# A decoder layer on one core: two small PSUM tiles drawn from another pool

## Chip, cores and metric

One core of a Trainium2 chip runs the whole kernel as one launch. The metric is the device time of that core in microseconds (us), the median of several executions. Beside it one execution was recorded by the hardware profiler; all rows below are from that one.

## What is computed

One inference step of one decoder layer, for a prompt of 1024 tokens of width 1024 and for 8 sample tokens. The layer has two mixers side by side, then cross-attention and a feed-forward part:

```python
def layer(l, x, mem_k, mem_v, shift0, wkv0):
    y_mix, chunk_v, shift_new, wkv_new = parallel_mixer(rmsnorm(x, ...), shift0, wkv0, ...)
    x = x + y_mix
    x = x + cross_attn(rmsnorm(x, norm_x_g[l]), mem_k, mem_v, w_xq[l], w_xo[l])
    x = x + sq_relu_ffn(rmsnorm(x, norm_ffn_g[l]), w_up[l], w_down[l])
```

The change touches mixer B, a recurrence with a 64 by 64 state for each of 8 heads, whose outputs are normalised per head, given a bonus term and gated:

```python
def step(S, inp):
    r_t, d_t, k_t, v_t, kk_t, a_t = inp
    sa = jnp.einsum('bhvk,bhk->bhv', S, -kk_t)
    S = S * d_t[:, :, None, :] + sa[..., None] * (kk_t * a_t)[:, :, None, :] + v_t[..., None] * k_t[:, :, None, :]
    return S, jnp.einsum('bhvk,bhk->bhv', S, r_t)
yb = headnorm(yb, ln_g, ln_b, GN_EPS)
out_b = ((yb + bonus).reshape(bsz, L, D_B) * g)
```

## The kernel before

Phase 1 is both mixers, phase 2 the output projection, the attention and the feed-forward part. In phase 1 the prompt is taken in two halves of 512 tokens, and the 8 heads of mixer B in four pairs (`pr`), two pairs at a time (`q`). A half has 8 chunks of 64 tokens (`NCH`, `C`), and the recurrence is solved chunk by chunk with small products.

For each half and pair the stages are, by name:

- `rkv`, `kknorm` (tile `pss`), `decay` (tiles `psw`, `psa`) and `factors` make the scaled operands `st` and `bk`. The ScalarE step at L446 reads `psa` into `ta`, which has one buffer; the VectorE step at L472 in `factors` is the last reader of the previous `ta`.
- `gram` (L478) multiplies `bk` with `st` in two groups of four chunks. Each group needs two tiles `psgram` at once; VectorE reads one at L499 and the other at L502. A gram cannot start before `bk` is written (L473 on VectorE, L474 on GpSimd).
- `inverse`, `join` (tiles `ps_j`), `ends` (`pse`) and `values` (`psv`) follow; `join` gives `tt`.
- `fold` (L615) runs twice for each pair: 32 TensorE products of 64 by 64 into one tile `psf`, then two copies out of it. The first fold (`i` = 0) rewrites the chunk ends, the second (`i` = 1) rewrites half of `ab`, copied by ScalarE twice (L626).
- `chain` walks the state through the chunks (`psx`, `psz`).
- `outs` (L651) sums the outputs in two tiles `psy`, which are open from the first chunk of the chain to the last, and which VectorE then reads (L669, L671).
- `gn` (L686) is the output norm: after a ScalarE square (L693) and a reciprocal root (L155 to L158), GpSimd scales `y` (L697), TensorE transposes it into the tile `psgn` (L700), ScalarE reads that (L702), GpSimd adds the bonus (L703), TensorE makes the gate in the tile `psgate` (L705), and VectorE multiplies (L706).

PSUM has eight banks, and a tile here takes one. In phase 1 they are shared out as pools: `pg` (two, tag g: the large projections and some transposes), `pm` (two, tag m), `pc` (two, the chain) and `py` (two, tag y). `pm` serves `pss`, `psw`, `psa`, `psgram`, `ps_j1` and `ps_j2`. `py` serves `psb`, `psv`, `pse`, `ps_j3`, `psf`, `psy`, `psgn`, `psgate` and a few sample tiles. A tile whose pool has no free slot waits until the last reader of an older one is done.

The stages are written in the list `ORDER` (L39), which gives their priority. The context is opened with `schedule_with_timeline_sim=True` (L1659): a planner takes the priorities and a simulated timeline, lets work whose data and slot are there go ahead, and fixes one order of instructions for each engine. Each engine then works in that order. The part of `ORDER` around the first of the places discussed reads:

```python
chain 0 0 6 8, outs 0 0, proj_a 0 1 1, fold 0 1 1, factors 0 2, mix_a 0 0,
x_store 1 0, decay 0 3, norm_a 0 1, gram 0 2, outs 0 1, factors 0 3, gram 0 3, x_store 1 1, gn 0 0
```

The arguments are half, pair (or `q`), and a part: `fold 0 1 1` is the second fold of pair 1 in half 0.

Of the kernel before, what the change touches and what calls it, by code (L numbers as in the profile page):

```python
# [9 lines left out]
F32 = mybir.dt.float32  # L10
# [9 lines left out]
P = 128  # L20
# [8 lines left out]
C = 64  # L29
NCH = HALF // C  # L30
# [40 lines left out]
class K:  # L71
# [543 lines left out]
    def fold(self, hf, pr, i):  # L615

        nc, t = self.nc, self.s[pr]
        tt = t["tt"]
        ps = self.py.tile([P, NCH, C], F32, tag="y", name="psf")
        hrs = (slice(0, 64), slice(64, 128))  # L620
        dsts = [t["e"][hr, 0:NCH, h, :] if i == 0 else t["ab"][hr, :, C:] for h, hr in enumerate(hrs)]
        for c in range(NCH):
            for hr, dst in zip(hrs, dsts):
                nc.tensor.matmul(ps[hr, c, :], tt[hr, c, :], dst[:, c, :], start=True, stop=True)
        for h, (hr, dst) in enumerate(zip(hrs, dsts)):
            self.copy((("vector", "scalar"), ("scalar", "scalar"))[i][h])(dst, ps[hr])  # L626
# [59 lines left out]
    def gn(self, hf, pr):  # L686
        nc, s1, s2 = self.nc, self.s1, self.s2
        t = self.s[pr]
        y = t["y"]
        y3 = y.rearrange("p (g v) -> p g v", v=64)  # L690
        sq = self.sl.tile([P, HALF], F32, tag="gs", name="gs")
        v, rs, tmp = (s1.tile([P, 8], F32, tag=f"gn{n}", name=f"gn{n}") for n in ("v", "r", "t"))
        nc.scalar.activation(sq, y, AF.Square)  # L693
        nc.vector.tensor_reduce(v, sq.rearrange("p (g v) -> p g v", v=64), axis=AX.X, op=ALU.add)
        nc.vector.tensor_scalar(v, v, 1.0 / 64, GN_EPS, op0=ALU.mult, op1=ALU.add)
        self.rsqrt(v, rs, tmp)
        nc.gpsimd.tensor_tensor(y3, y3, rs.unsqueeze(2).broadcast_to([P, 8, 64]), op=ALU.mult)  # L697
        ps = self.py.tile([P, 4, P], F32, tag="y", name="psgn")
        for c in range(4):
            nc.tensor.transpose(ps[:, c, :], y[:, c * P:(c + 1) * P], self.ident)  # L700
        psf = ps.rearrange("p c t -> p (c t)")
        nc.scalar.activation(y, psf, AF.Identity, scale=self.g["rw_ln_g"][:, pr:pr + 1], bias=self.g["rw_ln_b"][:, pr:pr + 1])  # L702
        nc.gpsimd.tensor_tensor(y, y, t["bv"], op=ALU.add)  # L703
        psg = self.py.tile([P, 512], F32, tag="y", name="psgate")
        nc.tensor.matmul(psg, self.g2[:, pr * P:(pr + 1) * P], self.s["G0"], start=True, stop=True)  # L705
        nc.vector.tensor_tensor(y, y, psg, op=ALU.mult)  # L706
        nc.sync.dma_start(self.d_o[hf][4 + pr], y)
# [955 lines left out]
```

## Time and profile before

| | |
|---|---|
| median of 3 executions | 1791.45 us (1782.59 to 1793.16) |
| the profiled execution, its own time | 1794.84 us |
| its span, first to last instruction | 1793.1 us |
| mean granted TensorE clock | 0.949 of full speed |
| TensorE busy | 1634.6 us, 91% of the span |
| VectorE busy | 1221.3 us, 68% |
| GpSimd busy | 837.1 us, 47% |
| ScalarE busy | 781.1 us, 44% |

The profile writes PE for TensorE, PEld for its weight loads, DVE for VectorE, ACT for ScalarE, POOL for GpSimd and SP for SyncE; L624 is line 624 of the kernel. An arrow out<-in names the tile written and those read. A row of the timeline may merge several like instructions (x30). Behind a group or a row in square brackets stands the idle time of the engine ahead of it and what ended it.

### The profile page before, as it was taken

Reading aid. Unit: us, or ns where it says so; the run is one execution under the profiler, and the core shown is the slowest. Engines: PE = TensorE matmul, PEld = TensorE weight load, DVE = VectorE, ACT = ScalarE, POOL = GpSimd, SP = SyncE. Lnnn points to the kernel's source line nnn. Section 1 sums busy time; section 2 is a strip of 40 time slices with the busy share of each in tenths; the row PEclk is TensorE's granted clock in tenths of the full one; section 3 lists DMA queues with packets and bytes.
Section 4 is the critical chain, followed back from the end, with each engine's and each line's share of the span. In section 5 each row is a group of like instructions: output and inputs, shape, how many; then the busy total and the mean of one; then the engine's idle time right before and its main releaser. Section 6 shows DMA issues by size and latency. Waiting matters only on the chain. (4 is left out here: it accounts for less than half of the span.)

```text
span 1793.1 us, 38347 instructions
## 1 busy us (share of the span) xinstructions
PE 1634.6 (91%) x15379; PEld 1521.9 (85%) x15379; DVE 1221.3 (68%) x2300; ACT 781.1 (44%) x1467; POOL 837.1 (47%) x643
## 2 busy tenths in 40 slices
PE   6989868998897689998999889999999999999997
PEld 6878757886786578887988789999999989999997
DVE  5586687768757965656667365655655697877796
ACT  4535543455443234433344233444544564444442
POOL 5450152323146864466343178687754533222343
PEclk8999978999898889999999999999999999999998
DMA  4411423221122456555455342567644585555442
GB/s 139 118 37 58 124 69 93 83 57 52 53 76 73 131 172 196 174 169 175 144 184 165 139 130 82 167 201 225 195 155 142 186 281 184 156 142 153 137 125 107
DMA packets 248547, 244.28 MB, mean 136 GB/s; under 512 B 24937, under 2 KB 191233, under 8 KB 248369
## 3 DMA queue, kind: packets, MB, share of 16 engines
q1 hardware_dynamic: 248324, 241.82, 44.1%
q8 instruction: 121, 1.98, 0.5%
q14 instruction: 58, 0.47, 0.1%
q10 hardware_dynamic: 44, 0.01, 0.0%
HBM read 179.95 MB, written 61.83 MB: 135 GB/s over the span
## 5 line engine op out<-in xcount | busy, mean ns | idle before, releaser
L104 POOL TENSOR_TENSOR wl<-wst,wh 128x1024 fp32r<-128x1024 f32 x70 | 170.3, 2433 | 125.6 <-ACT wh L103 112.1
L1215 PE MATMUL ps_S<-c_o,wS 128*128 128x258 f32 x1536 | 226.4, 282 | 0.0
L1215 PE MATMUL ps_S<-c_cb,wS 128*128 128x258 f32 x1536 | 226.0, 282 | 0.0
L136 PE MATMUL ps_g<-xh,wh 128*128 128x256 f32 (+1 forms) x704 | 214.6, 305 | 5.4 <-ACT xr L288 1.8
L136 PE MATMUL ps_g<-xl,wh 128*128 128x256 f32 (+1 forms) x704 | 209.6, 298 | 0.5 <-DVE xl L104 0.5
L136 PE MATMUL ps_g<-xh,wl 128*128 128x256 f32 (+1 forms) x704 | 207.7, 296 | 0.0
L1215 PEld LDWEIGHTS ps_S<-c_cb,wS 128*128 128x128 f32 x1536 | 201.8, 189 | 0.0
L1215 PEld LDWEIGHTS ps_S<-c_o,wS 128*128 128x128 f32 x1536 | 201.8, 189 | 0.0
L136 PE MATMUL ps_g<-o,wh 128*128 128x260 f32 (+1 forms) x768 | 178.0, 325 | 14.5 <-DVE yq L1240 8.9
L1215 PE MATMUL ps_A<-c_cb,wA 128*128 128x258 f32 x1152 | 173.0, 284 | 7.6 <-ACT c_cb L103 3.9
L1215 PE MATMUL ps_A<-c_o,wA 128*128 128x258 f32 x1152 | 172.7, 284 | 0.0
L1215 PEld LDWEIGHTS ps_A<-c_cb,wA 128*128 128x128 f32 x1152 | 153.4, 190 | 8.8 <-ACT c_cb L103 4.3
L1215 PEld LDWEIGHTS ps_A<-c_o,wA 128*128 128x128 f32 x1152 | 153.2, 190 | 0.4 <-DVE c_o L104 0.4
L103 ACT CAST wh<-wst 128x1024 fp32r<-128x1024 f32 x92 | 96.1, 1046 | 130.5 <-PE ps_g L136 63.9
L136 PEld LDWEIGHTS ps_g<-o,wh 128*128 128x128 f32 x768 | 129.2, 191 | 27.6 <-issue 9.2
L136 PEld LDWEIGHTS ps_g<-xh,wh 128*128 128x128 f32 x704 | 140.3, 199 | 12.9 <-issue 5.0
L136 PEld LDWEIGHTS ps_g<-xl,wh 128*128 128x128 f32 x704 | 139.9, 199 | 5.6 <-issue 2.2
L136 PEld LDWEIGHTS ps_g<-xh,wl 128*128 128x128 f32 x704 | 139.2, 198 | 3.0 <-issue 1.4
L1171 POOL TENSOR_TENSOR rS<-wr,rS 128x512 f32<-128x512 f32 x48 | 70.4, 1467 | 121.9 <-DMA wr<-in_w_down_dram 61.7
L136 PE MATMUL ps_g<-o,wl 128*128 128x260 f32 (+1 forms) x384 | 123.5, 322 | 1.4 <-POOL wl L104 1.4
L103 ACT CAST wS<-rS 128x512 fp32r<-128x512 f32 x96 | 59.3, 620 | 144.1 <-POOL rS L1171 84.1
L104 DVE TENSOR_TENSOR wS<-rS,wS 128x512 fp32r<-128x512 f32 x96 | 81.9, 853 | 46.6 <-ACT wS L103 46.3
(493 smaller groups left out, 3877.2 us busy)
## 6 DMA issues: line engine op xcount, KB each, us to landing
hb<-d_h SPq DMA_DIRECT2D x105, 258.0 KB
wst<-in_w_in_dram SPq DMA_DIRECT2D x44, 512.0 KB
d_h<-ht SPq DMA_DIRECT2D x64, 258.0 KB
wr<-in_w_down_dram SPq DMA_DIRECT2D x26, 512.0 KB
d_h<-yq SPq DMA_DIRECT2D x48, 258.0 KB
wst<-in_w_out_dram SPq DMA_DIRECT2D x16, 512.0 KB
ck<-in_cache_mem_k_dram SPq DMA_DIRECT2D x32, 256.0 KB
ck<-in_cache_mem_v_dram SPq DMA_DIRECT2D x32, 256.0 KB
```

The lines of the kernel that those rows point to most:

```text
L103: (heng or nc.scalar.copy)(hi, src)
L104: (eng or nc.vector).tensor_tensor(lo, src, hi.bitcast(F32), op=ALU.subtract)
L136: nc.tensor.matmul(ps, l[:, k, :], r[:, cols], start=(k == 0 and i == 0), stop=(k == kt - 1 and i == 2))
L1171: nc.gpsimd.tensor_tensor(R[n], R[x], R[y], op=op)
L1215: nc.tensor.matmul(ps[:, s], l[:, i, :], r[:, c, cols], start=k == 0 and j == 0, stop=k == 3 and j == 2)
```

## The change

Two tiles are taken from another pool: `psf` of the second fold, and `psgn` of the output norm, from `pm` in place of `py`. The first fold stays in `py`, and so does `psgate`. Nothing else is edited; no instruction is added or removed. There are 8 such folds and 8 such norms.

```diff
@@ fold
-        ps = self.py.tile([P, NCH, C], F32, tag="y", name="psf")
+        ps = (self.pm if i else self.py).tile([P, NCH, C], F32, tag="m" if i else "y", name="psf")
@@ gn
-        ps = self.py.tile([P, 4, P], F32, tag="y", name="psgn")
+        ps = self.pm.tile([P, 4, P], F32, tag="m", name="psgn")
```

## Rows read from the trace of the kernel before

**Rows 1.** The page, busy time, share of the span and instructions of each engine.

```profile
PE 1634.6 (91%) x15379; PEld 1521.9 (85%) x15379; DVE 1221.3 (68%) x2300; ACT 781.1 (44%) x1467; POOL 837.1 (47%) x643
```

**Rows 2.** Windows: stretch, length, busy time of PE, PEld, DVE, ACT, POOL, clock, DMA.

```profile
80.00:745.00 665.00, 573.49 (x7092) 498.30 (x7091) 480.52 (x1118) 298.16 (x580) 274.17 (x233) 0.90 0.31 92
745.00:1793.00 1048.00, 999.21 (x7890) 966.78 (x7888) 696.77 (x1091) 445.63 (x822) 520.69 (x339) 0.99 0.53 165
```

**Rows 3.** Waits of PE over the span: total us, times, longest.

```profile
PE psgn L700 <- DVE y L671: 10.7, 1, 10.7
PE psf L624 <- DVE y L671: 9.5, 1, 9.5
PE psf L624 <- DVE gnsm L670: 9.4, 1, 9.4
...
PE psgate L705 <- ACT y L702: 4.9, 1, 4.9
```

**Rows 4.** Windows of the three longest of these waits, columns as before.

```profile
226.80:236.20 9.40, 0.04 (x2) 0.00 (x0) 9.21 (x16) 2.59 (x4) 6.77 (x9) 0.50 0.23 66
...
562.60:572.10 9.50, 0.05 (x2) 0.02 (x1) 9.31 (x13) 2.55 (x3) 9.22 (x8) 0.57 0.24 74
...
580.80:591.50 10.70, 0.05 (x3) 0.05 (x1) 9.92 (x12) 0.63 (x1) 9.85 (x8) 0.66 0.08 31
```

**Rows 5.** Timeline of PE, 178 to 185 us.

```profile
179.88 0.50 PE L430 MATMUL psa<-L,dw 128*128 128x512 f32 x1
```

**Rows 6.** Timeline of all engines, around the fold at 236 us.

```profile
235.01 0.69 ACT L446 ACTIVATE ta<-psa,prm_derived 128x512 f32<-128x512 f32 x1 [1.73 <-DVE kkn L472]
...
236.08 0.69 DVE L473 SCALAR_TENSOR_TENSOR bk<-kkn,il 128x512 f32<-128x512 f32 x1
...
236.24 1.87 PE L624 MATMUL psf<-ab,tt 64*64 64x64 f32 x30 [9.40 <-DVE gnsm L670]
...
237.80 0.48 PE L498 MATMUL psgram<-st,bk 64*64 64x128 f32 x2
...
238.44 1.15 ACT L626 COPY ab<-psf 64x512 f32<-64x512 f32 x2
...
241.39 0.17 DVE L157 SCALAR_TENSOR_TENSOR gnt<-gnt,gnv 128x8 f32<-128x8 f32 x1 [1.48 <-ACT gnt L156]
```

**Rows 7.** Timeline of all engines, 572 to 595 us.

```profile
571.88 0.69 DVE L473 SCALAR_TENSOR_TENSOR bk<-kkn,il 128x512 f32<-128x512 f32 x1
...
573.84 0.67 PE L498 MATMUL psgram<-st,bk 64*64 64x128 f32 x4
...
576.57 1.17 ACT L626 COPY ab<-psf 64x512 f32<-64x512 f32 x2
...
581.53 2.38 DVE L470 SCALAR_TENSOR_TENSOR st<-kkn,lam 64x512 f32<-64x512 f32 x2 [1.63 <-ACT lam L451]
...
591.26 0.67 DVE L499 TENSOR_TENSOR ab<-psgram,mask 128x512 f32<-128x512 f32 x1
...
591.48 1.09 PE L700 MATMUL psgn<-ident,y 128*128 128x128 f32 x4 [10.65 <-DVE y L671]
...
592.50 2.62 PE L498 MATMUL psgram<-st,bk 64*64 64x128 f32 x32
...
592.66 0.78 ACT L702 ACTIVATE y<-psgn,prm 128x512 f32<-128x512 f32 x1 [11.22 <-POOL bk L474]
...
594.52 0.69 DVE L499 TENSOR_TENSOR ab<-psgram,mask 128x512 f32<-128x512 f32 x1 [0.83 <-PE psgram L498]
```

**Rows 8.** Timelines of PE and of ACT, 412 to 423 us.

```profile
412.78 0.63 PE L700 MATMUL psgn<-ident,y 128*128 128x128 f32 x4
...
414.15 1.10 PE L498 MATMUL psgram<-st,bk 64*64 64x128 f32 x30
420.19 2.07 PE L705 MATMUL psgate<-G,g 128*128 128x512 f32 x2 [4.95 <-ACT y L702]
```

```profile
419.38 0.76 ACT L702 ACTIVATE y<-psgn,prm 128x512 f32<-128x512 f32 x1
```

## The prediction, made before the changed kernel ran

> **What bounds the kernel now.** I read the busy shares first, then the windows, then the waits of TensorE, and last the timeline around each wait. The busy shares say that TensorE carries the span at 91% and VectorE follows at 68% [rows 1]. The windows say where TensorE has room. From 745 us on it is busy 999 of 1048 us, at a clock of 0.99, and the change touches nothing there. Between 80 and 745 us, the bulk of the mixers, it is busy 573.5 of 665 us: 91.5 us idle, at a clock of 0.90, while VectorE is busy 480.5 us [rows 2]. So only the mixers can answer to this change, and neither engine fills them: they alternate.
>
> The list of waits names the spots. The three longest waits of TensorE in the whole span are one norm transpose (10.7 us) and two second folds (9.5 and 9.4 us), all ended by VectorE's reading of an outputs tile `psy` [rows 3]. Neither product reads `psy`; it needs the slot. `outs` keeps both slots of `py` open until L671, and the second fold of the next pair, or the norm, stands behind it at the head of TensorE's order. The change is aimed at 29.5 us of waits (9.40 + 9.46 + 10.65 in the timeline rows). A fourth wait belongs to it too: 4.9 us of `psgate`, for the slot that `psgn` holds until ScalarE reads it.
>
> The question is what TensorE would do in those 29.5 us. VectorE is busy in 9.21 of 9.40, 9.31 of 9.50 and 9.92 of 10.70 us of them [rows 4]. The wait for a slot is thus the visible end of a queue on VectorE; the next product in line must be seen to need something else before the 29.5 us count as a gain.
>
> By the Trainium skill (Perfetto Trace Analysis, Identifying Performance Opportunities) improving the most-contended engine is what pays. Over the span that is TensorE, and by that reading all 29.5 us would be won; over the three stretches it is VectorE, and next to nothing would be. The rows above speak for the second reading.
>
> **The change, part by part.** No instruction, DMA or semaphore wait of another kind is added; two tiles change pool, and the planner may order every engine's queue of phase 1 anew. I cost the places one by one with the order otherwise kept.
>
> *The second fold at 236 us.* In `pm` one slot is held by `psa` from 179.88 us [rows 5] until ScalarE reads it at 235.01 to 235.70 [rows 6]; that leaves the other for the fold. Its operands are old, so it runs long before, in TensorE's busy stretch, and its cost there is its own 1.9 us (32 products), which leave the later place. At 236 us the gram is then first. It needs `bk`, which VectorE writes until 236.77; it starts near 236.8 in place of 237.80, so the idle time of 9.40 us turns into one of about 10 us in front of another product. What is won is the 1.0 us between, and on ScalarE the two copies of 1.15 us, which are done earlier. VectorE waits 1.48 us at 241.39 for ScalarE's root; with the copies out of the way it waits some 1.1 us less. Gain 1.1 us; bounds 0 (the copies hidden after all) and 1.9 us (the whole fold).
>
> *The second fold at 572 us.* The same pattern. `bk` is there at 572.57 and the gram began at 573.84; the copies take 1.17 us ahead of the exponentials for which VectorE waits 1.63 us at 581.53 [rows 7]. Gain 1.2 us; bounds 0 and 2.0.
>
> *The norm at 591 us.* The wait of 10.65 us does not go away. Both slots of `pm` hold the gram's first group, which VectorE begins to read at 591.26; its slot is free at 591.93, against 591.48 for the slot in `py` [rows 7]. Worse, the gram's second group needs two slots, and `psgn` sits in one until ScalarE is through: 591.95 plus the transposes (1.09 us at the low clock) plus the read (0.78 us) is 593.8, against a start at 592.50. VectorE then stands 0.83 us before the second group already; that grows by 1.3 us. Cost 1.3 us; bounds 0 (the gram put first) and 2.4 us (0.45 of the later slot and 1.95, the time from the transposes' start to the read's end in the rows).
>
> *The gate at 420 us.* `psgn` is written at 412.78 and read only at 419.38 to 420.14, because ScalarE's queue stands before it [rows 8]. In `pm` it leaves `py` free for the gate, whose two products then run near 414 us. But the gram, of which 30 of 32 products ran at 414.15, has one slot instead of two and waits for 420.14. The products after it begin after 1.1 to 1.9 us of gram, where before it was 2.07 us of gate and the last two of the gram. Gain about 1.2 us on TensorE; bounds: a loss of 1.1 us (the gram pushed back and nothing won) and a gain of the whole wait, 4.95 us.
>
> *The other twelve tiles.* None appears among the waits of [rows 3]. I cost them at nothing; what hides them is other TensorE work in the same stretch. If that cover is missing each may cost or give up to a pair of copies, 1.15 us [rows 6]; with signs mixed I keep 4 us to either side.
>
> Sum: 1.1 + 1.2 - 1.3 + 1.2 = 2.2 us gained. The profiled execution had 1794.84 us, its span plus 1.7 us around it, and would have 1792.6. It stood 3.4 us above the median, so against the median of 1791.45 the forecast is 1789 us. The bounds added up: losses of 0, 0, 2.4, 1.1 and 4 make 7.5, gains of 1.9, 2.0, 0, 4.95 and 4 make 12.9, so 1779 to 1799 with the order kept.
>
> **The rivals.**
>
> *Products fill the idle time (faster).* The planner, no longer bound to put the fold behind the outputs, places projections there, which need neither slot nor VectorE to start. For it: 91.5 us of idle TensorE, of which 29.5 are here, and the clock is at 0.50 in the first of these stretches [rows 4], its lower level of 1.2 GHz, so that filling them would also spare slow products afterwards. Against it: what `ORDER` has next there (gram, the next outputs) hangs on VectorE, and projections must be evacuated by VectorE too. The full price is 29.5 us, so 1762 us; half filled, 1777.
>
> *The norm stands in the gram's slot (slower).* A gram needs both slots of `pm` and a norm takes one. It happens where norms and grams overlap: the norms of pairs 0 to 3 in half 0 and of pair 0 in half 1, five of eight. It costs the time from the transposes to the end of ScalarE's read: 7.36 us at 412 us [rows 8], 1.95 at 591 us, and at least 0.6 + 0.8 for the other three, together 13.5 us. To this come the folds' copies if a second fold stays right ahead of a gram: 1.8 us at 236 us (the copies end at 239.59, the gram had begun at 237.80 [rows 6]), as much again at 572, so 17 us and 1808. It decides when the planner puts the norm first although ScalarE is late, which is what the row at 412 us shows; it is harmless if the gram's two groups go first. In its favour: gram, inverse, join, fold and chain follow each other, so a late gram is late for the whole half.
>
> A rule of the Trainium skill speaks for it (Perfetto Trace Analysis, Optimizing Tensor Performance, Matmuls): independent groups of products should rotate through different banks, so that the reading of one overlaps the next. Here two users of both kinds meet in two banks, and the rule would lead one to expect the loss above. The trace shows the price of such a meeting in `py` as 4.95 us once.
>
> *Nothing moves.* The planner's timeline may already have had the slot free where the chip had not, and then it keeps the old order: only the 2.2 us of my sum are at stake. That lies inside the forecast.
>
> **How the numbers follow.** A measurement of this kernel can tell about 1%, 18 us, from no change. The forecast, with rest and order about as they are (1779 to 1799), has 0.6. The filled idle time has 0.22, mostly between its half and its whole price, so 0.19 below 1773.5. The norm in the gram's slot has 0.18, of which 0.12 above 1809, since a planner that reorders can lose more than the sum. That gives faster 0.19, same 0.69, slower 0.12. The range takes in half and more of each rival: 1767 to 1808.
>
> **What would show it.** Right: the two waits of `psf` are gone from the list of waits, and the gram stands at the end of idle times of like length (8 to 10 us) ended by VectorE's L473; VectorE's busy share in these stretches stays near 98%; the stretch from 745 us to the end keeps its length. Wrong toward faster: projections `ps_g` inside the former waits and TensorE idle time between 80 us and the end of the mixers down from 91.5 to some 65 us. Wrong toward slower: new waits of `psgram` ended by ScalarE's L702 or L626. What would break the forecast most is an order that differs widely from the old one, since every place was costed with it kept.

## The result and the profile after

The changed kernel is slower by 1.1%, some 20 us. Its median is 1811.24 us (1807.37 to 1815.41, 6 executions) against 1791.12 us (also 6); the ratio is 1.0109, 95% interval 1.0086 to 1.0132. The forecast was 1789 us, a gain of 2.2 us, and its range ended at 1808. The ratios below compare undisturbed executions only, so one is not always the quotient of two medians. The profiled execution had 1807.37 us, the shortest of the six, a span of 1805.6 us and a clock of 0.943; that of the kernel before had 1794.84 us. So the two traces show 12.5 us of the loss.

The windows of the changed kernel, columns as in [rows 2]:

```profile
80.00:745.00 665.00, 563.36 (x6901) 486.32 (x6900) 462.10 (x1083) 283.46 (x557) 254.03 (x223) 0.89 0.30 89
226.80:236.20 9.40, 5.39 (x92) 4.75 (x92) 9.11 (x19) 5.79 (x9) 6.06 (x7) 0.68 0.31 71
240.00:330.00 90.00, 76.44 (x1085) 67.05 (x1082) 64.24 (x172) 31.89 (x62) 23.27 (x23) 0.80 0.29 86
330.00:430.00 100.00, 97.77 (x836) 85.71 (x832) 56.73 (x153) 48.94 (x101) 20.32 (x27) 0.96 0.22 63
560.00:690.00 130.00, 84.28 (x1275) 72.19 (x1274) 96.50 (x185) 35.16 (x68) 86.99 (x67) 0.79 0.44 128
745.00:1805.00 1060.00, 1018.75 (x8077) 984.36 (x8075) 707.59 (x1126) 452.72 (x840) 535.10 (x350) 0.98 0.53 165
```

The same stretches of the kernel before, where they were not shown:

```profile
240.00:330.00 90.00, 75.49 (x1185) 66.93 (x1182) 70.95 (x184) 35.97 (x72) 27.87 (x27) 0.87 0.31 92
330.00:430.00 100.00, 94.50 (x857) 81.06 (x856) 73.81 (x170) 54.72 (x108) 34.69 (x37) 0.97 0.21 60
560.00:690.00 130.00, 94.08 (x1393) 81.99 (x1391) 96.17 (x179) 46.45 (x84) 89.13 (x67) 0.83 0.54 157
```

Read the first stall first. From 226.8 to 236.2 us TensorE had 0.04 us of work [rows 4] and now has 5.39, while VectorE is as full as before, 9.11 of 9.40 us. Then read VectorE downwards: 6.7 us less work done in 240 to 330 us, 17.1 less in 330 to 430. TensorE is no less busy there than before, though in 240 to 330 us it gets through fewer products (1085 against 1185). VectorE has less to do in the middle of the mixers, and between 80 and 745 us it does 18.4 us of work less (462.10 against 480.52). That is not yet the loss: in 320 to 400 us, where VectorE is busy 40.59 us now and was 54.99, it is busy 43.50 us in e1 and 41.10 us in e8 below, and both lose nothing. Last, in 560 to 690 us, TensorE is idle 9.8 us more than before.

The waits of TensorE over the span, changed kernel:

```profile
PE ps_j L584 <- DVE pt L567: 12.7, 3, 7.0
PE ps_kvt L997 <- DVE kvt L992: 12.7, 5, 6.5
PE psgram L498 <- DVE ab L499: 9.9, 3, 4.8
PE ps_g L136 <- DVE yq L1240: 8.8, 5, 3.9
PE psy L663 <- DVE y L671: 8.6, 1, 8.6
PE psb L511 <- DVE zv L526: 5.4, 1, 5.4
```

The three long waits of [rows 3] are gone. What took their place is shorter and spread: the gram behind VectorE's read of its own tile, `outs` behind `psy`, `join` behind the inverse, the memory's transposes (`ps_kvt`) behind their copy.

The timeline of TensorE, with three rows of VectorE, at the places that the experiments below take up, changed kernel:

```profile
227.50 0.69 DVE L473 SCALAR_TENSOR_TENSOR bk<-kkn,il 128x512 f32<-128x512 f32 x1
...
240.87 1.69 PE L705 MATMUL psgate<-G,g 128*128 128x512 f32 x2
...
247.07 1.02 PE L705 MATMUL psgate<-G,g 128*128 128x512 f32 x2
...
254.88 0.60 PE L700 MATMUL psgn<-ident,y 128*128 128x128 f32 x4
...
256.17 0.60 PE L700 MATMUL psgn<-ident,y 128*128 128x128 f32 x4
...
261.11 0.68 DVE L706 TENSOR_TENSOR y<-y,psgate 128x512 f32<-128x512 f32 x1
...
261.87 0.68 DVE L706 TENSOR_TENSOR y<-y,psgate 128x512 f32<-128x512 f32 x1
...
261.97 0.60 PE L523 MATMUL psv<-ident,v 128*128 128x128 f32 x4
...
416.12 0.60 PE L700 MATMUL psgn<-ident,y 128*128 128x128 f32 x4
416.48 0.48 PE L430 MATMUL psw<-L,dw 128*128 128x512 f32 x1
...
606.23 1.06 PE L700 MATMUL psgn<-ident,y 128*128 128x128 f32 x4
607.22 1.97 PE L498 MATMUL psgram<-st,bk 64*64 64x128 f32 x30
...
611.05 0.36 PE L136 MATMUL ps_kv<-xh,wh 128*128 128x256 f32 x1
...
731.60 0.49 PE L136 MATMUL ps_g<-o,wh 128*128 128x260 f32 x2
```

Three patterns are new. Both gates of pairs 0 and 1 are written 14.0 and 9.1 us before their norms (240.87 and 247.07 against 254.88 and 256.17), and their two slots, all that `py` has, are free only after VectorE's multiplications at 261.11 and 261.87; `psv` comes at 261.97, when the first of them is done. Before, each gate followed its norm, and `psv` came at 262.72, so against the kernel before it is not late; against e1 below, where it comes at 258.00, it is. At 416 us `psw`, the first product of half 1 in `pm`, comes right behind the last norm of half 0; before, it ran at 374.60. And the gram that began at 573.84 [rows 7] stands behind the norm of pair 0 of half 1 and begins at 607.22.

All three have one root. The order in which the tiles of `pm` are first written by TensorE was taken from the trace and laid beside the list `ORDER`, for `pss`, `psw`, `psa`, `psgram`, `psgn` and the sample's `ps_sa`. In both kernels the two agree from the first tile to the last, and so they do with `psf` added. In these kernels the planner lets work go ahead across pools, not within `pm`: the pool is a queue in the order of the program. `ORDER` there reads "gn 0 2, rkv 1 1 0, gn 0 3, decay 1 0" and "decay 1 3, gn 1 0, proj_a 1 2 0, sample_update 0, gram 1 2".

### The profile page after: what moved, and what is told of

It is laid out like the page before. It is cut to its first block, busy times and chain, and to the rows that moved or that the text cites. A ratio compares the mean times of both kernels' runs of the same rounds, so it can differ in the third digit from the quotient of the medians.

```text
span 1805.6 us, 38322 instructions
## 1 busy us (share of the span) xinstructions
PE 1644.5 (91%) x15379; PEld 1528.2 (85%) x15379; DVE 1213.9 (67%) x2300; ACT 774.0 (43%) x1463; POOL 831.4 (46%) x643
## 5 line engine op out<-in xcount | busy, mean ns | idle before, releaser
L136 PEld LDWEIGHTS ps_g<-xh,wh 128*128 128x128 f32 x704 | 140.1, 199 | 17.1 <-ACT wh L103 5.4
```

The costliest lines, as they stand in the source:

```text
L136: nc.tensor.matmul(ps, l[:, k, :], r[:, cols], start=(k == 0 and i == 0), stop=(k == kt - 1 and i == 2))
```

## Experiments

Each kernel is told by its edit against the kernel before or the changed one. Where a line is added or the list is one line shorter, line numbers shift by one (L701 for L700, L699 for L700). A trace is of one execution, a ratio of all of them.

### Which half of the change

**e1, folds alone.** The second fold in `pm`, the norm left in `py`.

> Only the second fold's tile is taken from pm; the norm's stays in py. Theory Q (the pool is a queue in the order of the program: the norms of pairs 2 and 3 of half 0 stand in pm ahead of the decay of half 1, so that its products psw wait for them, 416.5 us against 374.6 before): psw of half 1 starts near 375 us, the stretch 320 to 400 us has VectorE busy some 55 us again, and the time is 1780 to 1795 us. Rival F (the folds' slot is what costs: the early fold sits ahead of the sample's tile ps_sa, which came at 375.8 in place of 335.5): psw stays near 410 and the time is 1805 to 1815. Rival N (any new order of the planner lands within 1% by chance): no such pattern, the time is not tied to where psw stands.

Ratio 0.9996 (0.9971 to 1.0020). `psw` came at 388.33 and not near 375, and VectorE is busy 43.50 us in 320 to 400 us, not some 55. So two signs of Theory Q are missing, and still there is no loss; VectorE's lag in that stretch does not make one by itself. There is no gain either, although the waits of 9.40 and 9.46 us are gone here too. Rival F falls.

**e2, norms alone.** The norm in `pm`, the folds left in `py`.

> Only the norm's tile is taken from pm; the second fold's stays in py. Theory Q: psw of half 1 starts after the second norm of half 0, near 415 us, VectorE is busy some 40 of 80 us in 320 to 400, and the time is 1805 to 1820 us; the three-fold gain of some 9 us near 236 us that the folds brought is missing. Rival F: 1788 to 1795 us, psw near 375.

Ratio 1.0127 (1.0065 to 1.0189, 4 executions), with `psw` at 414.99. The norms carry the whole loss.

### Which norms

The edit in e3 to e6, e10 and e11 chooses the pool by half and pair:

```diff
-        ps = self.py.tile([P, 4, P], F32, tag="y", name="psgn")
+        inpm = (hf, pr) in ((0, 2), (0, 3))
+        ps = (self.pm if inpm else self.py).tile([P, 4, P], F32, tag="m" if inpm else "y", name="psgn")
```

**e3, three norms taken back.** The changed kernel, `inpm = (hf, pr) not in ((0, 2), (0, 3), (1, 0))`.

> As the changed kernel, but the norms of three pairs go back to py: pairs 2 and 3 of half 0 (ahead of the decay of half 1 in the program) and pair 0 of half 1 (ahead of the gram of pair 2 of half 1, which began 33 us later than before). The other five norms and all second folds stay in pm. Theory Q: the loss is gone, psw near 375 us, gram of pair 2 of half 1 near 575, the time 1778 to 1795 us. Rival F: the time stays at 1805 to 1815. Rival N: anything between.

Ratio 1.0093 (1.0059 to 1.0127): nearly all of the loss stays, although `psw` moved to 398.17 and the gram to 583.78. Theory Q had named the wrong norms.

**e4, two norms.** The kernel before with the condition as printed above.

> As the kernel before, but two tiles go to pm: the norms of pairs 2 and 3 of half 0. Theory Q: these two alone bring the loss of 320 to 430 us, psw near 415, the time 1803 to 1815 us. Rival F: as before, 1788 to 1795 us, psw near 375.

Ratio 1.0004 (0.9984 to 1.0025). `psw` did move, by 32 us, as Theory Q said; but alone that costs nothing.

**e5, the first two norms.** `inpm = (hf, pr) in ((0, 0), (0, 1))`, on the kernel before.

> As the kernel before, but two tiles go to pm: the norms of pairs 0 and 1 of half 0. Theory G (the gate overtakes its norm: the norms then stand in pm behind the grams of pairs 2 and 3, their gates in py do not, take both slots of py some 10 us before the norms run, and hold them until the multiplication by the gate; the values and ends of pairs 2 and 3 wait for py): last product of the ends of pair 2 and 3 near 280 us in place of 274.7, VectorE less busy between 320 and 430 us than before, the time 1800 to 1812 us. Theory Q (only norms of pairs 2 and 3 of half 0, ahead of the decay of half 1, cost): 1788 to 1795 us.

Ratio 1.0078 (1.0054 to 1.0102): the larger part of the loss of e2, some 14 us (0.78% of 1791). The products of which the expectation speaks, near 280 us, are the ends of pair 2; those of pair 3 come later.

**e6, the norms of half 1.** `inpm = hf == 1`, on the kernel before.

> As the kernel before, but four tiles go to pm: the norms of half 1. Theory G: the gate of a norm can overtake it here too, but TensorE has projections of the memory to fill in: 1790 to 1800 us, the first 400 us as before. Theory Q: the norm of pair 0 holds up the gram of pair 2 (574 us before) by some 10 us; 1795 to 1805 us. If the loss of the five other norms sits here and not in pairs 0 and 1 of half 0: 1803 to 1815 us.

Ratio 1.0050 (1.0026 to 1.0074), 1800.1 us: Theory Q's range. **e10** takes only the first of them, `(hf, pr) == (1, 0)`, and **e11** the other three.

> As the kernel before, but one tile goes to pm: the norm of pair 0 of half 1. The four norms of half 1 together cost 0.5%, and the gram of pair 2 began 13 us later. Theory Q (the norm holds up the gram behind it in pm): this one norm brings the whole 0.5%, 1796 to 1803 us, gram of pair 2 near 587 us. Rival G1 (the gates of pairs 1 to 3 overtake their norms late in the half): as before, 1788 to 1793 us.

> As the kernel before, but three tiles go to pm: the norms of pairs 1, 2 and 3 of half 1. Theory Q: as before, 1788 to 1793 us, since nothing in pm stands behind them that hurries. Rival G1: 1796 to 1803 us.

e10: 1.0048 (1.0027 to 1.0068). e11: 0.9995 (0.9968 to 1.0023). The whole cost of half 1 is one tile. Timeline of TensorE in e10:

```profile
589.62 1.06 PE L701 MATMUL psgn<-ident,y 128*128 128x128 f32 x4
590.61 0.69 PE L498 MATMUL psgram<-st,bk 64*64 64x128 f32 x4
```

The gram begins 16.8 us later than in [rows 7] (590.61 against 573.84), right behind the norm. But that is its first group, which in the kernel before lay in its slots until VectorE read it at 591.26 [rows 7]. The reads of VectorE in e10:

```profile
592.57 0.69 DVE L499 TENSOR_TENSOR ab<-psgram,mask 128x512 f32<-128x512 f32 x1 [0.96 <-PE psgram L498]
...
616.64 0.69 DVE L817 TENSOR_REDUCE sy<-stmp 128x8 f32<-128x512 f32 x1 [8.49 <-POOL stmp L816]
617.25 0.68 DVE L499 TENSOR_TENSOR ab<-psgram,mask 128x512 f32<-128x512 f32 x1
```

and the last of them before:

```profile
605.50 0.68 DVE L499 TENSOR_TENSOR ab<-psgram,mask 128x512 f32<-128x512 f32 x1
```

The first read is 1.3 us late, the last, of the gram of pair 3, 11.8. Ahead of it VectorE's new order has a sum for the sample tokens (`sy`), for which it stands 8.49 us until GpSimd has written the operand; GpSimd itself stood 4.27 us for a transfer. The `join` behind that gram begins 11.7 us later (649.56 against 637.91), and the products on `o` that open phase 2 come 11.8 us later (725.21 against 713.46). The same wait, of 9.60 and 9.45 us, stands ahead of the last read in e6 and e2; in the kernel before, in e11 and in the changed kernel no wait for `sy` stands there. So in this execution of e10 most of the time is lost where the planner put another task of VectorE ahead. No run moves `sy` alone, so this is read from the traces and not shown by an edit. The gate of this pair runs ahead of its norm too (582.20 against 589.62), but `psv` and `psb` in `py` behind it come earlier than before (588.74 and 592.44 against 596.02 and 598.70).

All norms together, from the parts: 0.78 + 0.48 + 0.04 - 0.05 = 1.25%, against 1.27% in e2. Set on the kernel before, the parts add up, as far as intervals of 0.2 to 0.6% to either side can tell.

### Is it the gate?

**e9.** e5, with the gates of the same two pairs in `pm` as well.

```diff
-        psg = self.py.tile([P, 512], F32, tag="y", name="psgate")
+        psg = (self.pm if inpm else self.py).tile([P, 512], F32, tag="m" if inpm else "y", name="psgate")
```

> As the kernel before, but the norms of pairs 0 and 1 of half 0 and their gates go to pm, four tiles. The norms alone cost 0.78% here. Theory G (the loss is the gate's overtaking: it holds both slots of py while its norm waits in pm): with the gate behind its norm in the same queue the loss is gone, 1786 to 1795 us, and the last product of the ends of pairs 2 and 3 is back at 275 us or earlier. Rival Q1 (the loss is the norm's late start behind the grams, whatever the gate does): 1800 to 1808 us.

Ratio 1.0008 (0.9977 to 1.0039): the loss of e5 is gone. Timelines of TensorE, e5 first:

```profile
250.32 2.07 PE L706 MATMUL psgate<-G,g 128*128 128x512 f32 x2
...
253.03 1.60 PE L706 MATMUL psgate<-G,g 128*128 128x512 f32 x2
...
259.86 0.60 PE L701 MATMUL psgn<-ident,y 128*128 128x128 f32 x4
...
261.16 0.60 PE L701 MATMUL psgn<-ident,y 128*128 128x128 f32 x4
...
266.52 0.60 PE L523 MATMUL psv<-ident,v 128*128 128x128 f32 x4
```

then e9:

```profile
255.46 1.65 PE L523 MATMUL psv<-ident,v 128*128 128x128 f32 x8
...
263.66 0.60 PE L701 MATMUL psgn<-ident,y 128*128 128x128 f32 x4
...
265.40 1.02 PE L706 MATMUL psgate<-G,g 128*128 128x512 f32 x2
...
266.85 0.66 PE L701 MATMUL psgn<-ident,y 128*128 128x128 f32 x4
```

In e9 the norms run even later than in e5, and nothing is lost: Rival Q1 falls. What differs is that `py` is free, so that `psv` runs at 255.46 and not at 266.52. The ends of pair 2 began at 261.32 in place of 270.95, as foretold; those of pair 3 began 4.5 us later than in e5, which was not. So that the gate moves with its norm takes the loss away is shown; that the late `psv` is its path is not. The `join` of these pairs begins at 285.33 in e5, at 285.50 in e9 and at 285.96 before, and the first fold of pair 2 at 315.57, 316.89 and 313.08. Nor can the two traces show it: the profiled execution of e5 took 1798.42 us, the shortest of its six, and that of e9 1797.27.

**e7, all gates in `pm`,** on the changed kernel: `psg = self.pm.tile(...)`.

> As the changed kernel, but the gate's tile goes to pm as well, so that norm and gate stand in one queue and the gate cannot take a slot before its norm. Theory G: py is free for the values, whose transposes run near 255 us in place of 262; what the gates cost in pm is 2 us of TensorE each ahead of a gram or a decay; if the overtaking carries most of the loss, the time is 1788 to 1800 us. Theory Q: the norms of half 0 still hold up psw, and the gates behind them hold it up some 5 us more: 1810 to 1825 us.

Ratio 1.0039 (1.0012 to 1.0065), 1798 us: two thirds of the loss gone, at the upper end of Theory G's forecast and against Theory Q. `psv` runs at 242.33.

### The order of the program

**e8** is the changed kernel with steps of `ORDER` moved, and **e12** the kernel before with the same moves:

```diff
-sample_a, values 1 0, gn 0 2, rkv 1 1 0, gn 0 3, decay 1 0, rkv 1 1 1, kknorm 1 0
+sample_a, values 1 0, decay 1 0, kknorm 1 0, gn 0 2, rkv 1 1 0, gn 0 3, rkv 1 1 1
-decay 1 3, gn 1 0, proj_a 1 2 0, sample_update 0, gram 1 2
+decay 1 3, proj_a 1 2 0, sample_update 0, gram 1 2, gn 1 0
```

> As the changed kernel, but in the order of the program the decay and the key norm of pair 0 of half 1 come ahead of the norms of pairs 2 and 3 of half 0, and the norm of pair 0 of half 1 behind the gram of pair 2. Theory Q: psw of half 1 near 380 us in place of 416.5, VectorE busy over 65 us again in 330 to 430 (56.7 in the changed kernel), the gram near 575, and the time 1785 to 1798 us. Theory G: psw earlier as said, but the 10 us lost at 240 to 280 us stay: 1800 to 1808 us.

> As the kernel before, both pools untouched, with the order of the program that took the whole loss from the changed kernel (decay and key norm of pair 0 of half 1 ahead of the norms of pairs 2 and 3 of half 0, norm of pair 0 of half 1 behind the gram of pair 2). Theory Q: norms and decays stand in different pools here, so the order has little to undo: within 0.4% of before, 1784 to 1797 us. Rival O (the order is a gain of its own, which covers a loss that is still there in the changed pools): 1768 to 1782 us.

e8: 0.9994 (0.9975 to 1.0012), with `psw` at 396.83 (foretold near 380) and VectorE busy 64.57 us in 330 to 430 us (foretold over 65). e12: 0.9993 (0.9969 to 1.0018). The order gives back the whole loss, and is worth nothing where the norms stand in `py`: the times are Theory Q's in both, and Rival O falls. But by e5 the gate's 0.78% should have stayed in e8, where the first two gates still run ahead of their norms (240.88 and 247.09 against 254.89 and 256.18) and `psv` comes at 261.98. So the two halves were taken apart, on the changed kernel: **e13** only the norm behind the gram, **e14** only decay and key norm ahead of the norms.

> As the changed kernel, with one step moved in the order of the program: the norm of pair 0 of half 1 behind the gram of pair 2. Theory A (the parts add up): the 0.48% of this norm goes, the rest of 1.09% stays: 0.6% above before, 1799 to 1805 us, gram of pair 2 near 590 us in place of 607. Theory B (the loss at 240 us is made up for as soon as nothing else holds half 1 up): all goes, 1788 to 1795 us.

> As the changed kernel, with two steps moved in the order of the program: decay and key norm of pair 0 of half 1 ahead of the norms of pairs 2 and 3 of half 0. Theory A: these two norms cost nothing by themselves, so 0.9 to 1.1% above before stay, 1805 to 1812 us. Theory C (after the late gates the slack of these norms is used up, and psw at 416.5 us counts): the 0.48% of the other norm stays and the rest goes, 1796 to 1803 us, psw near 398 us.

e13: 1.0118 (1.0092 to 1.0145). e14: 1.0041 (1.0021 to 1.0060). Theory A fails twice, and Theory B with e13. The norm behind the gram gives back nothing alone, though the gram moved from 607.22 to 580.24 as it should; together with the other move it gives back another 0.5% (e14 to e8). Theory C fits e14. So the parts add up on the kernel before and not on the changed one. Its cause is not settled.

**e15** is e8 with the gates in `pm`, **e16** is e1 with the order of e8.

> As the changed kernel, with the gate's tile in pm as well and both moves of the order: decay and key norm ahead of the norms of pairs 2 and 3 of half 0, norm of pair 0 of half 1 behind the gram. Theory A: gate cured (0.7%) and norm cured (0.48%), nothing of the loss is left and perhaps a little is won: 1780 to 1792 us. Rival: VectorE and the pool are full, four users of two slots in pm cost 0.3% as before: 1793 to 1800 us.

> As the kernel before, with only the second folds in pm and both moves of the order. The folds alone and the order alone each changed nothing. Every theory so far: 1784 to 1795 us; if the 8 us that the folds win at 238 us are given back only because the start of half 1 does not follow, it is 1778 to 1786 us.

e15: 1.0047 (1.0027 to 1.0068), 1801 us, just above the rival's range: the order on top of the gate's cure wins nothing over e7. Read against e8 it says more: with the order mended, taking the gates into `pm` too costs 0.5%. So the gate's place next to its norm is no cure by itself. e16: 0.9990 (0.9963 to 1.0018); the 8 us that the folds win at 238 us are not to be had this way.

### Where the time is realised

In phase 1 TensorE has a filler for the last mixers, the projections of the memory (`ps_kv`); the products on `o` that open phase 2 use the same pool `pg` and come behind them in the program. The first `ps_kv` and the first product on `o`, from the timelines, with the time of the profiled execution itself, all in us:

| kernel | ratio | profiled execution | first `ps_kv` | first on `o` |
|---|---|---|---|---|
| before | 1 | 1794.8 | 600.8 | 713.5 |
| e2 norms alone | 1.0127 | 1819.6 | 609.3 | 740.3 |
| e13 norm behind gram | 1.0118 | 1811.5 | 606.1 | 733.5 |
| changed | 1.0109 | 1807.4 | 611.0 | 731.6 |
| e3 three taken back | 1.0093 | 1804.8 | 609.8 | 731.6 |
| e5 first norms | 1.0078 | 1798.4 | 604.5 | 730.2 |
| e10 one norm | 1.0048 | 1805.1 | 595.9 | 725.2 |
| e15 gate and order | 1.0047 | 1802.4 | 572.6 | 717.8 |
| e14 decay ahead | 1.0041 | 1793.9 | 571.6 | 709.4 |
| e9 norms and gates | 1.0008 | 1797.3 | 596.2 | 715.7 |
| e8 whole order | 0.9994 | 1790.1 | 573.9 | 714.2 |
| e1 folds alone | 0.9996 | 1789.6 | 580.4 | 706.0 |

The five slowest by ratio open phase 2 at 730 us or later, all others, also those not in the table, before 726. e5 stands out: its profiled execution opens phase 2 late and is only 3.6 us longer than that of the kernel before. In the changed kernel the last gate ends 17.4 us later (761.5 against 744.1), the opening of phase 2 is 18.1 us late, and the span 12.5 us longer. So in these two traces the loss is there when phase 2 opens, and is not made after it.

Where it arises on the way there, in four kernels (start of the first fold of pair 2 in half 0, of the first gram and the first fold of half 1, of its last `join`, and of phase 2, in us):

| kernel | fold, half 0 | gram, half 1 | fold, half 1 | last `join` | phase 2 |
|---|---|---|---|---|---|
| before | 313.1 | 414.1 | 506.4 | 637.9 | 713.5 |
| e1 folds alone | 309.3 | 416.6 | 501.5 | 638.9 | 706.0 |
| changed | 313.5 | 435.1 | 517.5 | 658.6 | 731.6 |
| e8 whole order | 311.8 | 436.2 | 509.0 | 647.7 | 714.2 |

At 313 us the changed kernel is level with the one before: with the late gates it has lost the 4 us that e1 is ahead, and no more. It falls 21 us behind at the first gram of half 1, has half of that back at the first fold, and is 21 us behind again at the last `join`. e8 has the same late gram and makes it up.

**e17** (on the kernel before) and **e18** (on the changed kernel) let the filler begin earlier:

```diff
-mem_load, mix_a 1 2, ends 1 3, inverse 1 1
+mem_load, mix_a 1 2, memkv 0 0 2, ends 1 3, inverse 1 1
```

> As the kernel before, with one step moved in the order of the program: the first two chunks of the memory's projections right behind the mix of head 2 of half 1, ahead of ends, inverse and join. Theory M (what counts is when this filler gets going, since TensorE is idle 32 of 80 us in 560 to 640): ps_kv begins near 575 us in place of 601, and the next phase near 700 in place of 713.5; 1775 to 1787 us. Rival (VectorE is the bound of that stretch and each chunk asks 0.84 us of it): 1787 to 1798 us.

> As the changed kernel, with the same step moved. Theory M (the late filler carries the loss): the loss goes or nearly so, ps_kv begins near 580 us in place of 611, the next phase near 712 in place of 731.6, 1785 to 1797 us. Rival (the mixers themselves are late by 17 to 20 us and set the end, whatever fills them): 1803 to 1814 us.

e17: 0.9968 (0.9942 to 0.9995), 1786 us: `ps_kv` from 559.75, phase 2 from 712.25 and not near 700. That is a shade faster than the kernel before, the only kernel here whose interval lies below 1; among eighteen kernels an interval that ends at 0.9995 is weak evidence. e18: 1.0037 (1.0016 to 1.0058), `ps_kv` from 577.25, phase 2 from 718.28. The move is worth 0.3% before and 0.7% in the changed kernel: each theory holds in part, and with these intervals the two sizes are hardly told apart. Of the loss of 1.1%, 0.7% remain against e17. An early filler alone does not decide either: e14 and e15 begin it near 572 us and are 0.4 to 0.5% slower than the kernel before.

The windows of 560 to 690 us, e18:

```profile
560.00:690.00 130.00, 97.18 (x1382) 85.57 (x1382) 100.78 (x199) 38.89 (x75) 94.04 (x69) 0.84 0.47 140
```

With the filler early TensorE is busy 97.2 us there, not 84.3, and VectorE does 4.3 us more. So VectorE was not full in that stretch of the changed kernel, and the late filler left TensorE idle there.

## Why the prediction was wrong, step by step

**VectorE is full in the stalls, so removing them wins nothing: right in its result.** Where the first wait was, VectorE is at 9.11 of 9.40 us after, 9.21 before. The folds alone remove waits of 9.40 and 9.46 us and move the time by -0.04%. The picture behind it did not come true: no idle time of like length in front of the gram took the place of the wait (the longest wait of a gram for `bk` is 2.9 us). VectorE wrote `bk` at 227.50 to 228.19 and not until 236.77, and TensorE worked 5.39 us there. Nor did the stretch from 745 us to the end keep its length: it is 1060 us in place of 1048, since phase 2 opens late. By the reading over the whole span of the Trainium skill's rule (Perfetto Trace Analysis, Identifying Performance Opportunities), which the prediction set aside, these 18.9 us would be won, and e1 would be 1.05% faster; the measurement speaks against that reading.

**The order otherwise kept: the step that failed.** The prediction costed each place "with the order otherwise kept" and named a widely different order as what would break it most; it gave the twelve other tiles 4 us to either side. What it missed stood in `ORDER`: the tiles of `pm` are served in the order of the program. Moving a tile to another pool moves it to another queue, and so changes its neighbours: `psw` of half 1 went from 374.60 to 416.48, behind the last norm, and the gram of pair 2 from 573.84 to 607.22. That the loss hangs on this order is shown: with the pools of the changed kernel and three steps of `ORDER` moved, e8 is at 0.9994 in place of 1.0109, while the same moves on the kernel before change nothing (e12).

**The other twelve tiles at nothing: wrong by some 14 us.** The norms of pairs 0 and 1 of half 0 are among them and cost 0.78% alone, on the kernel before (e5). What happens there was in neither the sum nor the rivals: the norm went behind the grams of pairs 2 and 3, and the gate stayed in `py`, went ahead of its norm and held a slot, in the changed kernel until 261.8 us. With the gate in the same queue nothing is lost (e9). By which path the early gates cost time is open, and in e8, where they are as early, no loss is left.

**The norm at 591 us: the right place and side, another wait.** Cost 1.3 us, bounds 0 to 2.4; measured 0.48%, 8.6 us (e10). The working took the gram to be in its slots and the norm behind it, as in the rows of before. In the queue the norm of pair 0 is ahead, so the gram waits not for a read of 0.78 us but for the norm's own operands, and begins 16.8 us later. Even that is mostly hidden, since VectorE reads it only 1.3 us later than before. What is late in the trace of e10 is the last gram's read, 11.8 us, behind a wait of VectorE for GpSimd that the new order put there.

**The second folds, gains of 1.1 and 1.2 us:** within the noise, e1 shows none. They run early as said, and in the changed kernel the gram began 9 us earlier (228.82 against 237.80). In e1 4 us of that are left at the first fold of pair 2 (309.26 against 313.08), and none at the last `join`; why is not known.

**The gate at 420 us:** it runs at 409.60, before the 414 us of the forecast, but the 1.2 us cannot be told from nothing (e4, 1.0004). The gram that it should have held until 420.14 began at 435.07, because its decay stood behind both norms.

**The rivals.** "The norm stands in the gram's slot" had the side and nearly the size (1808 us), with 0.18; the size is luck. Its own sign, new waits of `psgram` ended by ScalarE's L702 or L626, is not in the changed kernel: the waits of `psgram` there (9.9, 3.9 and 2.6 us in total) are ended by VectorE. Of its five places the one at 591 us costs, but not by the 1.95 us of a read; the 7.36 us at 412 us cost nothing alone (e4); and the two of pairs 0 and 1, which it priced at 1.4 us each, carry most, by another mechanism. That products fill the idle time is half right: TensorE has 5.35 us more work in the first stall, and the kernel is no faster for it.

**What stays open:** why the parts that add up on the kernel before do not add up on the changed one (e13, e14, e8, e15), and by which path the late tiles cost time at the end. Rival N of e1, that any new order of the planner moves the time by chance, is not excluded for single kernels. Against it as the whole cause speaks that seven kernels with other orders (e1, e4, e8, e9, e11, e12, e16) lie within 0.1% of the kernel before; for it, that the wait found in e10 belongs to a task that the change did not touch.

## What to carry to other kernels

Where, as here, a planner serves the tiles of a pool in program order, write out the list of that pool's users around a tile before moving it there, and ask whom it now stands behind and who stands behind it. Mending the program's order can be worth more than moving more tiles (e8 against e7). A tile that is used with another may have to move with it, since a partner left in the old pool can go ahead and hold slots that others need; but try it, because it helped in e9 and e7 and cost 0.5% in e15. A new order can also cost on an engine that the change did not name. And a long wait for a slot is worth its length only if the engine that frees the slot is not itself the bound of that stretch.

## What was not expected of the hardware

In 240 to 330 us the granted clock fell from 0.87 to 0.80 in the changed kernel, with TensorE busy as long as before (76.4 against 75.5 us), on fewer products. It did not decide: e8 has 0.80 there too (windows below) and loses nothing.

```profile
240.00:330.00 90.00, 77.19 (x1086) 67.94 (x1082) 66.27 (x172) 31.88 (x62) 23.24 (x23) 0.80 0.29 86
```
